# One layer of a hybrid Fourier and neighbourhood-attention block: front-stage products, low halves and the first fold given to the vector engine alone

## The chip, the cores and the metric

The kernel runs on one core of a Trainium2 chip. The engines of that core are TensorE (PE in the profile: matrix products), VectorE (DVE), ScalarE (ACT), GpSimd (POOL) and SyncE (SP, which issues most DMAs). They run side by side and wait for each other through semaphores. The metric is the device time of one execution in microseconds (us).

## The reference

One layer, one batch, 1024 positions of 1024 channels, 256 context tokens, all in fp32. Condensed:

```python
sh_x, sc_x, g_x = split(silu(c)     @ w_ada + b_ada, 3)
sh_c, sc_c, g_c = split(silu(c_ctx) @ w_ada + b_ada, 3)
xn = rms_norm(x,   norm_g) * (1 + sc_x) + sh_x
cn = rms_norm(ctx, norm_g) * (1 + sc_c) + sh_c
fx_in, fx_gate, qx, kx, vx, nx_gate = split_proj(xn @ w_in)
_, _, _, kc, vc, _                  = split_proj(cn @ w_in)
f  = real(fft2(fx_in, over positions and group channels)) * (l * 128) ** -0.5
f_out  = (f @ w_four) * silu(fx_gate)
na_out = neighbourhood_attention(rms_norm(qx), rms_norm(kx), vx, rms_norm(kc), vc, rel_bias) * silu(nx_gate)
out = x + g_x * (concat(f_out, na_out) @ w_out)
```

## The kernel before, in words

Matrix products are made of fp32 numbers cut into a high half (`h`, type fp32r) and a low half (`l`, the remainder), so that each product is three matmuls: high by high, high by low, low by high.

**The front stage** is what the change touches. Eight position tiles `x` (128 x 1024) are normalised and turned by PE into eight channel tiles, kept in `xrt` (two tensors, four channel tiles each). For each channel tile i = 0..7 the shift `sh` and the scale `av` are needed. Each is a sum of products of a row tile of the turned `w_ada` with the activated condition: `wds[i, 0]` and `wds[i, 1]` (both named `wd`, 128 x 1024) against `sbc` (for x) and `scc` (for the context). So there are 16 such dot products for x (columns `colsx`) and 16 for the context (`colsc`). `ada_out` makes three tiny instructions of the two sums of a tile (L252 to L254), and `modulate` then makes high halves `xnh` (ACT, L371), the modulated tile itself (`xrt`, ACT or DVE) and low halves `xnl` (DVE, L374). `load_gate` and its `cut` load the gate weights `wr` (128 x 512) of channel tile i and cut them into halves, both named `w`: high on ACT (L207), low by a subtraction. `gate_products` feeds PE with 24 matmuls per channel tile (L380) into the eight PSUM banks `pg`. The halves of the gate weights have three buffers, so the halves of tile i + 3 wait until PE has done the 24 matmuls of tile i.

**The fold** follows. `fourier_gate` empties `pg` into `gate_f` (ACT, L477); `fold_weights` multiplies `wtr` by `cst` into the bank `pw`, which is split into `wab_h` (ACT) and `wab_l` (DVE, L114). `fold_ends(i)` adds and subtracts mirrored positions of channel tile i: two instructions of 128 x 512, `ef` and (in place) `od`. `fold_middle` folds each once more (four DVE instructions of 128 x 256, L535, into `s`), casts to `h` on ACT (L538) and takes the low half `l` on DVE (L541, the last one L546), one step late. `fold_ends(i + 2)` stands behind the middle fold of tile i. `fold_products` gives PE 26 matmuls per tile (L554 to L567). Then `turn_columns` and everything behind it (projections, attention, output) take over.

**What sets the order.** In the front stage a planner inside the kernel runs at build time: each step has one or more alternatives (engine, guessed duration, function), and is given to the first engine that is free by the planner's own clock; the order in which the functions are called is the order on each engine. From `fold_zero` on the order is written out by the program. The planner's clock is set to zero again behind the fold, so the later stages do not depend on what it did in front.

The touched lines are L236 and L237 (scratch tiles `sq`), `far_dot` (product on POOL L288, its sum on ACT L291, or both on DVE in `dot` L257), `cut` in `load_gate` (L334 or L335), and `fold_ends` (L514, L515).

Of the kernel before, what the change touches and what calls it, by code (L numbers as in the profile page):

```python
# [11 lines left out]
F32 = mybir.dt.float32  # L12
R = mybir.dt.float32r
AF = mybir.ActivationFunctionType
ALU = mybir.AluOpType
# [4 lines left out]
P = 128  # L20
DM = 1024
KT = 8
TC, RX, RG, RM = 3.0, 2, 0, 2
TW, RT0, RT1, RT2, RH, D0, D1, NC = 4, 0, 4, -1, 1, 0, 0, 0
# [20 lines left out]
def tile_hybrid_block(  # L45
# [26 lines left out]
    act, dve, pool, pe = nc.scalar, nc.vector, nc.gpsimd, nc.tensor  # L72
# [6 lines left out]
    def f(t):  # L79
        return t.bitcast(F32)  # L80
# [35 lines left out]
    def dma(o, i):  # L116
        nc.sync.dma_start(out=o, in_=i)


    PE_, ACT_, DVE_, POOL_ = "pe", "act", "dve", "pool"  # L120
# [7 lines left out]
    def clock():  # L128
        return now[0] if past[0] is None else past[0]

    def at(t, fn):
        heapq.heappush(events, (t, len(order), fn))
        order.append(0)

    def on(alts, then=None, rank=2):

        taken = []
        for eng, dur, fn, *more in alts:
            heapq.heappush(ready[eng], (rank, len(order), dur, fn, then, more, taken))
            order.append(0)  # L140
        for eng, *_ in alts:
            issue(eng)
# [17 lines left out]
    def chain(*ops, rank=2):  # L160


        def run(n=0):
            if n == len(ops):
                return
            op = ops[n]
            if callable(op):
                at(clock() + SEM, op)
                run(n + 1)
            elif isinstance(op, list):  # L170
                on(op, lambda: run(n + 1), rank)
            else:
                on([op[:3]], lambda: run(n + 1), op[3] if len(op) > 3 else rank)
        at(clock() + (2 * SEM if past[0] is None else 0), run)

    def arrive(t, kb, fn):

        free["dma"] = max(free["dma"], t + 1.0) + 0.3643 * kb
        at(free["dma"] + 1.0, fn)
# [24 lines left out]
    def copy_by(n, who, out, in_):  # L204

        both = ((DVE_, dve.tensor_copy, lambda n: 0.07 + n * 0.00052), (POOL_, pool.tensor_copy, p_t), (ACT_, act.copy, a_t))
        return [(e, time(n), lambda cp=cp: cp(out, in_)) for e, cp, time in (both[k] for k in who)]  # L207

    def when(keys_, fn):
        if has(*keys_):  # L210
            fn()
        else:
            at(clock() + 0.1, lambda: when(keys_, fn))

    def mark(*key):
        return lambda: done.__setitem__(key if len(key) > 1 else key[0], 1)
# [15 lines left out]
    wa = st2.enter_context(tc.tile_pool(name="wa", bufs=1, **LT))  # L232
    sbc = wa.tile([P, DM], F32, name="sbc")
    scc = wa.tile([P, DM], F32, name="scc")
    junk = wa.tile([P, DM], F32, name="junk")
    sq = [wa.tile([P, DM], F32, name=f"sq{k}") for k in range(2)]  # L236
    spare = list(sq)  # L237
    sqx = w4p.tile([P, DM], F32, tag="wr", name="sqx")
    xnst = ExitStack()
    xnp = xnst.enter_context(tc.tile_pool(name="xnp", bufs=1, **RT))  # L240
# [3 lines left out]
    def halves():  # L244

        t = pwp.tile([P, 1040], R, tag="w", name="w")
        return t[:, 0:512], t[:, 512:1024]
# [8 lines left out]
    def dot(wd, s, jk, col, scale=1.0):  # L256
        dve.tensor_tensor_reduce(out=jk, in0=wd, in1=s, scale=scale, scalar=0.0, op0=ALU.mult, op1=ALU.add, accum_out=col)  # L257
# [25 lines left out]

    def far_dot(wd, s, col, key, rank):

        def product():
            scrs.append(spare.pop(0) if key[0] == "x" else wd)
            pool.tensor_tensor(out=scrs[0], in0=wd, in1=s, op=ALU.mult)  # L288

        def total():  # L290
            act.activation(scrs[0], scrs[0], AF.Copy, accum_out=col)  # L291
            if key[0] == "x":
                spare.append(scrs[0])

        scrs = []
        alts = [(DVE_, 1.14, lambda: dot(wd, s, junk, col)),
                (POOL_, 2.3, product, (ACT_, 1.04, total))]
        chain(alts[D0] if key == ("x", 0, 0) else alts[D1] if key == ("x", 0, 1) else alts, mark(*key), rank=rank)

    def ada(i, s, dsh, dav, name, rank):  # L300
        cols = wa.tile([P, 2], F32, name=f"cols{name}{i}")
        for j in range(2):
            when(((name, "s"), ("wd", i, j) if name == "x" else ("x", i, j)), lambda j=j: far_dot(wds[i, j], s, cols[:, j:j + 1], (name, i, j), rank))
        when(((name, i, 0), (name, i, 1), "vec"), lambda: chain((DVE_, 0.27, lambda: ada_out(i, cols, dsh, dav)), mark(name, i), rank=rank))
# [22 lines left out]
    def load_gate(i):  # L327
        wr = wgp.tile([P, 512], F32, tag="wr", name="wr")
        dma(wr, w_in[i * P:(i + 1) * P, 0:512])

        def cut():
            gate_w[i] = wh, wl = halves()
            chain(copy_by(512, WHO["gc"], wh, wr), mark("wh", i),
                  [(DVE_, 0.6, lambda: dve.tensor_tensor(out=wl, in0=wr, in1=f(wh), op=ALU.subtract)),  # L334
                   (POOL_, 1.22, lambda: pool.tensor_tensor(out=wl, in0=wr, in1=f(wh), op=ALU.subtract))],  # L335
                  mark("wl", i), rank=RG + 10 * i)
        arrive(clock(), 2.0, lambda: when((("g", i - 3, 2, 1),) if i > 2 else (), cut))

# [171 lines left out]
    def fold_ends(i):  # L510
        xi = xrt[i // 4][:, i % 4]
        ef = eop.tile([P, 513], F32, tag="ef", bufs=EB, name="ef")
        od = xi[:, 1:513]
        pool.tensor_tensor(out=ef[:, 1:513], in0=xi[:, 1:513], in1=xi[:, 1023:511:-1], op=ALU.add)  # L514
        pool.tensor_tensor(out=od, in0=xi[:, 1:513], in1=xi[:, 1023:511:-1], op=ALU.subtract)  # L515
        act.mul(ef[:, 0:1], xi[:, 0:1], 2.0)
        folded[i] = (ef, od)

    def fold_middle():

        lows = []
        for i in range(KT):
            ef, od = folded[i]
            h4 = pwp.tile([P, 1040], R, tag="w", name="h4")[:, 0:1024].rearrange("p (a b) -> p a b", a=4)
            l4 = eop.tile([P, 4, 256], R, tag="l4", name="l4")
            folded[i] = (h4, l4)
            lo, hi = od[:, 0:256], od[:, 510:254:-1]
            folds = (
                ((ef[:, 1:257], ef[:, 511:255:-1], ALU.add), (ef[:, 0:256], ef[:, 512:256:-1], ALU.subtract)),
                ((lo, hi, ALU.subtract), (lo, hi, ALU.add)),  # L530
            )
            for z in range(2):
                s2 = eop.tile([P, 2, 256], F32, tag="s2", bufs=3, name="s2")
                for y, (u, v, op) in enumerate(folds[z]):
                    dve.tensor_tensor(out=s2[:, y], in0=u, in1=v, op=op)  # L535
                    yield
                h, l = h4[:, 2 * z:2 * z + 2], l4[:, 2 * z:2 * z + 2]
                act.copy(h, s2)  # L538
                lows.append(dict(out=l, in0=s2, in1=f(h), op=ALU.subtract))
                if len(lows) > LAG:  # L540
                    dve.tensor_tensor(**lows.pop(0))  # L541
                yield
            if i + EB < KT:
                fold_ends(i + EB)
        for low in lows:
            dve.tensor_tensor(**low)  # L546
            yield
# [32 lines left out]
    with tc.manual_schedule(engines=MANUAL):  # L580
        fold_zero()
        for i in range(EB):
            fold_ends(i)
# [754 lines left out]
    op = {}  # L1338
# [431 lines left out]
```

## Time and profile before

| what | value |
|---|---|
| three runs, median (lowest to highest) | 627.29 us (626.17 to 630.08) |
| the profiled execution | 624.08 us, its span 622.3 us |
| busy PE / DVE / ACT / POOL | 555.5 / 494.9 / 363.6 / 294.8 us |
| mean granted TensorE clock | 0.962 of full speed |

The span is what lies between the first and the last instruction; the profiled execution's own time is 1.8 us longer. A share of busy time is an average over stages with different limits. For a change to the front stage the first 160 us are what counts: the fold's last DVE instruction starts at 146.24 us.

### The profile page before, as it was taken

The page shows a single profiled execution, that of the slowest core. Times are in us where ns is not written, and L with a number is a line of the kernel's source. Part 1 is how long each engine was busy: PE and PEld are TensorE (multiplying, and loading weights), DVE is VectorE, ACT ScalarE, POOL GpSimd, SP SyncE. Part 2 cuts the span into 40 slices and gives each one's busy share as a digit, 9 for nine tenths or more (in the row PEclk, how much of TensorE's full clock was granted, in tenths as well). Part 3 has the DMA queues.
Part 4 walks back from the last instruction along what each step waited for, and adds up shares of the span by engine and source line. Part 5 has one row for each costly group of instructions (what it writes and reads, how often), then busy time and mean ns, then how long its engine had stood idle before and what let it go on. Part 6 is the DMA issues. An engine that isn't in the chain of part 4 may idle for free. (4 is left out here: it accounts for less than half of the span.)

```text
span 622.3 us, 8690 instructions
## 1 busy us (share of the span) xinstructions
PE 555.5 (89%) x2923; PEld 482.8 (78%) x2923; DVE 494.9 (80%) x926; ACT 363.6 (58%) x765; POOL 294.8 (47%) x230
## 2 busy tenths in 40 slices
PE   6588485969999999998999989999999798999997
PEld 3466264858977798897988979889898587788886
DVE  5999999999688968868787688886868969878242
ACT  6544165525554357786688777887778737754100
POOL 3657926571374463544344553344543737515300
PEclk9889598988999999999999999999999989999999
DMA  8960033401478524112113111132011746104142
GB/s 338 407 240 0 0 112 126 137 0 61 131 234 297 160 94 123 56 38 74 34 42 109 50 55 52 41 99 61 23 46 40 230 162 214 63 5 148 52 174 97
DMA packets 42889, 68.83 MB, mean 111 GB/s; under 512 B 3542, under 2 KB 25430, under 8 KB 42844
## 3 DMA queue, kind: packets, MB, share of 16 engines
q1 hardware_dynamic: 41836, 64.60, 30.8%
q0 software_dynamic: 1008, 3.67, 1.7%
q8 instruction: 23, 0.38, 0.3%
q14 instruction: 22, 0.18, 0.1%
HBM read 59.35 MB, written 8.91 MB: 110 GB/s over the span
## 5 line engine op out<-in xcount | busy, mean ns | idle before, releaser
L812 PE MATMUL pqkv<-wh,xnh 128*128 128x384 f32 x256 | 86.8, 339 | 0.0
L812 PE MATMUL pqkv<-wl,xnh 128*128 128x384 f32 x256 | 86.7, 339 | 0.0
L812 PE MATMUL pqkv<-wh,xnl 128*128 128x384 f32 x256 | 86.1, 336 | 0.0
L1185 DVE CUSTOM_DVE_ANT_0 pr<-s,bias 128x640 f32<-128x640 f32 (+1 forms) x64 | 50.4, 787 | 22.6 <-PE s L1180 16.7
L1189 ACT ACTIVATE pr<-pr,tr 128x640 f32<-128x640 f32 (+1 forms) x64 | 51.2, 801 | 27.3 <-DVE tr L1185 26.9
L718 POOL TENSOR_TENSOR hrs<-hss,mhalf 128x4 f32<-128x4 f32 (+1 forms) x34 | 37.7, 1112 | 59.7 <-DVE hss L715 52.0
L202 DVE TENSOR_TENSOR el<-e,eh 128x384 fp32r<-128x384 f32 (+2 forms) x71 | 51.8, 735 | 11.0 <-ACT eh L207 9.9
L202 POOL TENSOR_TENSOR wl<-wr,wh 128x384 fp32r<-128x384 f32 (+1 forms) x24 | 30.4, 1271 | 46.6 <-ACT wh L207 27.8
L202 POOL TENSOR_TENSOR el<-e,eh 128x512 fp32r<-128x512 f32 x25 | 32.5, 1302 | 41.4 <-ACT eh L207 41.3
L207 ACT CAST eh<-e 128x384 fp32r<-128x384 f32 (+2 forms) x96 | 49.4, 528 | 1.4
L812 PEld LDWEIGHTS pqkv<-wl,xnh 128*128 128x128 f32 x256 | 48.1, 188 | 1.4
L812 PEld LDWEIGHTS pqkv<-wh,xnh 128*128 128x128 f32 x256 | 48.1, 188 | 1.3
L812 PEld LDWEIGHTS pqkv<-wh,xnl 128*128 128x128 f32 x256 | 48.1, 188 | 0.7
L1281 ACT ACTIVATE e<-e 128x384 f32<-128x384 f32 (+1 forms) x64 | 31.5, 496 | 29.1 <-DVE e L1271 28.6
L380 PE MATMUL pg<-xnh,w 128*128 128x512 f32 x128 | 36.9, 446 | 11.5 <-ACT xnh L371 11.5
L380 PEld LDWEIGHTS pg<-xnh,w 128*128 128x128 f32 x128 | 27.7, 220 | 20.3 <-ACT xnh L371 13.9
L1271 DVE TENSOR_TENSOR e<-st,biast 128x256 f32<-128x256 f32 (+2 forms) x80 | 34.0, 444 | 7.7 <-PE st L1263 6.8
L1178 PE MATMUL s<-ks,qs 128*128 128x256 f32 (+1 forms) x128 | 30.2, 316 | 7.4 <-DVE tr L1185 7.0
L371 ACT ACTIVATE xnh<-xrt,sh,av 128x512 fp32r<-128x512 f32 x16 | 12.6, 808 | 38.7 <-DVE av L254 38.7
L1178 PEld LDWEIGHTS s<-ks,qs 128*128 128x128 f32 x128 | 23.3, 192 | 14.9 <-DVE tr L1185 11.7
L1262 PE MATMUL st<-qs,ks 128*128 128x512 f32 (+2 forms) x96 | 33.6, 353 | 0.3
L1263 PE MATMUL st<-qs,ks 128*128 128x512 f32 (+2 forms) x96 | 33.3, 347 | 0.0
(297 smaller groups left out, 1730.0 us busy)
## 6 DMA issues: line engine op xcount, KB each, us to landing
wd<-in_w_ada_t_dram SPq DMA_DIRECT2D x16, 512.0 KB, 9.0
wr<-in_w_in_dram SPq DMA_DIRECT2D x40, 192.0 KB, 2.8
wr<-in_w_in_dram SPq DMA_DIRECT2D x24, 256.0 KB, 3.7
x<-in_xb_dram SPq DMA_DIRECT2D x8, 512.0 KB, 6.6
wdg<-in_w_ada_t_dram SPq DMA_DIRECT2D x8, 512.0 KB, 4.1
owr<-in_w_out_dram SPq DMA_DIRECT2D x16, 256.0 KB, 3.1
y<-in_xb_dram SPq DMA_DIRECT2D x8, 512.0 KB, 6.2
out_dram<-y SPq DMA_DIRECT2D x15, 256.0 KB, 2.1
```

The costliest lines, as they stand in the source:

```text
L202: return [(e, time(n), lambda eng=eng: eng.tensor_tensor(out=out, in0=in0, in1=in1, op=op)) for e, eng, time in (both[k] for k in who)]
L207: return [(e, time(n), lambda cp=cp: cp(out, in_)) for e, cp, time in (both[k] for k in who)]
L380: mm(pg[j][hf], gate_w[i][w][:, j * P:(j + 1) * P], x[i][:, hs], start=(i == 0 and g == 0), stop=(i == KT - 1 and g == 2))
L718: lambda: pool.tensor_tensor(out=rs[:, 0:nh], in0=ss[:, 0:nh], in1=mhalf[:, 0:nh], op=ALU.pow),
L812: mm(o, x[k][:, ts_], w, start=(k == 0 and n == 0), stop=(k == KT - 1 and n == 2))
L1178: mm(o, qs1[h][:, ts_], ks1[h][:, kk], start=st, stop=sp)
L1185: dve.tensor_tensor_reduce(out=pr, in0=sv, in1=bt, scale=-1.0, scalar=3.0e38, op0=ALU.add, op1=ALU.min, accum_out=tr[:, t:t + 1])
L1189: (ACT_, a_t(nl + CTX) + 0.15, lambda: act.activation(pr, pr, AF.Exp, bias=tr[:, t:t + 1], scale=-1.0, accum_out=sm[:, t:t + 1])),
L1262: mm(s, ks1[h][:, kk], qs1[h][:, qq], start=True, stop=False)
L1263: mm(s, ks2[h][:, kk], qs2[h][:, qq], start=False, stop=True)
L1271: dve.tensor_tensor(out=ew[:, u:v], in0=s3[:, u:v], in1=mixes[p, h][0][:, blocks], op=ALU.add)
L1281: ops = [(DVE_, d_t(m), add), give, lambda: done.__setitem__(("add", p, h, kt), 1), (ACT_, a_t(m), lambda: act.activation(ew, ew, AF.Exp))]
```

## The change

All 32 dot products are made on DVE, as one fused instruction each (before, 16 of them were products on POOL followed by a sum on ACT). The low halves of all eight gate weight tiles are taken on DVE (before, two of them on POOL). The 16 instructions of the first position fold are made on DVE (before, on POOL). The two scratch tiles `sq` go away. Nothing else is edited; the planner then places some other steps differently.

```diff
-    sq = [wa.tile([P, DM], F32, name=f"sq{k}") for k in range(2)]
-    spare = list(sq)
...
     def far_dot(wd, s, col, key, rank):
 
-        def product():
-            scrs.append(spare.pop(0) if key[0] == "x" else wd)
-            pool.tensor_tensor(out=scrs[0], in0=wd, in1=s, op=ALU.mult)
-
-        def total():
-            act.activation(scrs[0], scrs[0], AF.Copy, accum_out=col)
-            if key[0] == "x":
-                spare.append(scrs[0])
-
-        scrs = []
-        alts = [(DVE_, 1.14, lambda: dot(wd, s, junk, col)),
-                (POOL_, 2.3, product, (ACT_, 1.04, total))]
-        chain(alts[D0] if key == ("x", 0, 0) else alts[D1] if key == ("x", 0, 1) else alts, mark(*key), rank=rank)
+        chain((DVE_, 1.14, lambda: dot(wd, s, junk, col)), mark(*key), rank=rank)
...
             chain(copy_by(512, WHO["gc"], wh, wr), mark("wh", i),
-                  [(DVE_, 0.6, lambda: dve.tensor_tensor(out=wl, in0=wr, in1=f(wh), op=ALU.subtract)),
-                   (POOL_, 1.22, lambda: pool.tensor_tensor(out=wl, in0=wr, in1=f(wh), op=ALU.subtract))],
+                  (DVE_, 0.6, lambda: dve.tensor_tensor(out=wl, in0=wr, in1=f(wh), op=ALU.subtract)),
                   mark("wl", i), rank=RG + 10 * i)
...
-        pool.tensor_tensor(out=ef[:, 1:513], in0=xi[:, 1:513], in1=xi[:, 1023:511:-1], op=ALU.add)
-        pool.tensor_tensor(out=od, in0=xi[:, 1:513], in1=xi[:, 1023:511:-1], op=ALU.subtract)
+        dve.tensor_tensor(out=ef[:, 1:513], in0=xi[:, 1:513], in1=xi[:, 1023:511:-1], op=ALU.add)
+        dve.tensor_tensor(out=od, in0=xi[:, 1:513], in1=xi[:, 1023:511:-1], op=ALU.subtract)
```

On POOL, from the reciprocal roots `rs` of the norm to the clearing of `a` behind the fold, this stands before (the first rows of each kind):

```order
L356 TENSOR_TENSOR rs<-ss,mhalf 128x1 x8
L335 TENSOR_TENSOR w<-wr,w 128x512
L288 TENSOR_TENSOR sq_105<-wd,sbc 128x1024
...
L288 TENSOR_TENSOR wd<-wd,scc 128x1024 x3
...
L514 TENSOR_TENSOR ef<-xrt_97 128x512
L515 TENSOR_TENSOR xrt_97<-xrt_97 128x512
```

and this is all that is left there in the changed kernel (`tab`: the transform's tables; `wf`: two sums of the Fourier weights):

```order
L341 TENSOR_TENSOR rs<-ss,mhalf 128x1 x8
L560 DMA tab<-in_tab_h_dram 128x1026
L560 DMA tab<-in_tab_l_dram 128x1026
L560 DMA tab<-in_tab_h_dram 128x1026
L560 DMA tab<-in_tab_l_dram 128x1026
L595 TENSOR_TENSOR wf<-wf 128x1024
L597 TENSOR_TENSOR wf<-wf 128x1024
L625 MEMSET a_1213 64x260
```

34 instructions are gone from POOL; the two sums of `wf` now follow the table loads directly.

On DVE, at the end of the context's dot products and the start of the fold, this stands before (`x0h`: position zero; a dot is the ISA row with `junk`, the ISA row behind it reads its sum):

```order
L257 ISA junk,colsc_430<-wd,scc 128x1024
L257 ISA colsc_430 128x1
...
L254 TENSOR_TENSOR avc<-colsc_430,vec 128x1
L535 TENSOR_TENSOR s_791<-ef 128x256 x2
L535 TENSOR_TENSOR s_798<-xrt_97 128x256 x2
L541 TENSOR_TENSOR l_790<-s_791,h_789 128x512
L535 TENSOR_TENSOR s_812<-ef 128x256 x2
```

and this in the changed kernel:

```order
L255 ISA junk,colsc_424<-wd,scc 128x1024
L255 ISA colsc_424 128x1
...
L252 TENSOR_TENSOR avc<-colsc_424,vec 128x1
L499 TENSOR_TENSOR ef<-xrt_97 128x512
L500 TENSOR_TENSOR xrt_97<-xrt_97 128x512
...
L520 TENSOR_TENSOR s_773<-ef 128x256 x2
L520 TENSOR_TENSOR s_780<-xrt_97 128x256 x2
L526 TENSOR_TENSOR l_772<-s_773,h_771 128x512
L499 TENSOR_TENSOR ef<-xrt_97 128x512
L500 TENSOR_TENSOR xrt_97<-xrt_97 128x512
```

All 16 dots of the context now stand on DVE behind the last dot for x and ahead of the first fold (before, seven of the 16 were on DVE at all), and the first folds stand between the middle folds.

On ACT, at channel tiles 1 to 3, with the engines that each row waits for, this stands before:

```order
L371 ACTIVATE xnh_119<-xrt_97,sh,av 128x16x4x8 [waits DVE_49]
L291 ACTIVATE sq_106,colsx_371<-sq_106 128x1024 [waits Pool_49]
L371 ACTIVATE xnh_119<-xrt_97,sh,av 128x16x4x8
L207 CAST w<-wr 128x512 [waits DMAHW6_49,PE_49]
L291 ACTIVATE sq_105,colsx_373<-sq_105 128x1024 [waits Pool_49]
L371 ACTIVATE xnh_120<-xrt_97,sh,av 128x16x4x8 [waits DVE_49]
```

and this in the changed kernel:

```order
L356 ACTIVATE xnh_117<-xrt_97,sh,av 128x16x4x8 [waits DVE_49]
L356 ACTIVATE xnh_117<-xrt_97,sh,av 128x16x4x8
L207 CAST w<-wr 128x512 [waits DMAHW6_49,PE_49]
L358 ACTIVATE xrt_97<-xrt_97,sh,av 128x16x32 [waits Activation_49]
L356 ACTIVATE xnh_118<-xrt_97,sh,av 128x16x4x8 [waits DVE_49]
```

The sums L291 are gone from ACT, and ACT now modulates 11 of the 16 half tiles of `xrt` itself (L358; before, three), behind a cast that waits for PE. The order on PE is the same in both kernels, and so is the order on all engines behind the fold.

## Rows read from the trace of the kernel before

**Rows 1.** Two stretches: busy us (instructions) by engine, granted TensorE clock, DMA share, GB/s.
```profile
22.00:147.00 125.00, 89.24 (x428) 73.12 (x427) 122.36 (x173) 56.07 (x106) 78.99 (x43) 0.84 0.30 106
61.00:82.00 21.00, 10.14 (x24) 6.43 (x24) 20.90 (x12) 4.81 (x8) 20.44 (x8) 0.59 0.07 25
```

**Rows 2.** DVE groups by form, 20 to 147 us: count, busy us, mean ns.
```profile
L374 DVE TENSOR_TENSOR xnl<-xrt,xnh 128x512 fp32r<-128x512 f32 x16 | 17.3, 1089 | 0.1
L252 DVE TENSOR_TENSOR sh<-colsx,vec 128x1 f32<-128x1 f32 x8 | 6.9, 863 | 0.0
```

**Rows 3.** POOL groups by form, 20 to 147 us.
```profile
L288 POOL TENSOR_TENSOR wd<-wd,scc 128x1024 f32<-128x1024 f32 x9 | 26.1, 2929 | 5.2 <-ACT scc L425 5.2
L514 POOL TENSOR_TENSOR ef<-xrt 128x512 f32<-128x512 f32 x8 | 12.9, 1610 | 26.7 <-DVE shc L252 15.3 <-DVE s L535 11.4
```

**Rows 4.** Timeline of POOL and DVE around 61 to 73 us: start, us.
```profile
61.62 19.82 POOL L288 TENSOR_TENSOR wd<-wd,scc 128x1024 f32<-128x1024 f32 x7
...
70.15 2.29 DVE L252 TENSOR_TENSOR sh<-colsx,vec 128x1 f32<-128x1 f32 x1
```

**Rows 5.** Timeline of DVE, 22 to 26 us.
```profile
22.02 0.08 DVE L257 DVE_READ_ACCUMULATOR2_ANT colsx<- 128x1 f32 x1
...
23.41 2.14 DVE L254 TENSOR_TENSOR av<-colsx,vec 128x1 f32<-128x1 f32 x1
```

**Rows 6.** Timeline of DVE, 88 to 93 us.
```profile
88.14 0.68 DVE L334 TENSOR_TENSOR w<-wr,w 128x512 fp32r<-128x512 f32 x1
88.74 0.68 DVE L374 TENSOR_TENSOR xnl<-xrt,xnh 128x512 fp32r<-128x512 f32 x1
89.35 0.15 DVE L252 TENSOR_TENSOR sh<-colsx,vec 128x1 f32<-128x1 f32 x1
...
89.73 0.15 DVE L252 TENSOR_TENSOR shc<-colsc,vec 128x1 f32<-128x1 f32 x1
...
91.65 1.22 DVE L257 CUSTOM_DVE_ANT_0 junk<-wd,scc 128x1024 f32<-128x1024 f32 x1
...
92.79 0.54 DVE L372 TENSOR_SCALAR xrt<-xrt,av,sh 128x512 f32<-128x512 f32 x1
```

**Rows 7.** Timeline of PE, 20 to 97 us: the gate products.
```profile
26.45 6.69 PE L380 MATMUL pg<-xnh,w 128*128 128x512 f32 x16 [4.28 <-ACT xnh L371]
32.98 2.03 PE L380 MATMUL pg<-xnl,w 128*128 128x512 f32 x8
...
50.84 3.90 PE L380 MATMUL pg<-xnh,w 128*128 128x512 f32 x16
...
56.43 3.83 PE L380 MATMUL pg<-xnh,w 128*128 128x512 f32 x16
```

**Rows 8.** Timeline of DVE and POOL, 127 to 135 us: the middle fold.
```profile
127.23 0.75 DVE L535 TENSOR_TENSOR s<-ef 128x256 f32<-128x256 f32 x2
127.90 0.68 DVE L541 TENSOR_TENSOR l<-s,h 128x512 fp32r<-128x512 f32 x1
...
131.10 2.52 POOL L610 TENSOR_TENSOR wf<-wf 128x1024 f32<-128x1024 f32 x1
131.34 2.83 DVE L541 TENSOR_TENSOR l<-s,h 128x512 fp32r<-128x512 f32 x1
```

**Rows 9.** Timeline, 106 to 114 us: fold weights.
```profile
108.88 1.08 ACT L477 ACTIVATE gate_f<-pg 128x512 f32<-128x512 f32 x2
...
111.42 1.35 POOL L515 TENSOR_TENSOR xrt<-xrt 128x512 f32<-128x512 f32 x1
...
111.55 2.47 DVE L114 TENSOR_TENSOR wab_l<-pw,wab_h 128x512 fp32r<-128x512 f32 x4
```

**Rows 10.** Timeline of DVE and PE at the fold's end.
```profile
146.24 0.69 DVE L546 TENSOR_TENSOR l<-s,h 128x512 fp32r<-128x512 f32 x1
...
152.41 0.28 PE L669 MATMUL pp<-onesr,a 34*4 34x258 f32 x1
```

**Rows 11.** PE in two stretches of the fold: busy us (matmuls), granted clock, DMA share, GB/s.
```profile
135.00:138.00 3.00, 3.00 (x16) 0.50 0.00 0
145.00:150.00 5.00, 5.00 (x43) 1.00 0.00 0
```

## Prediction

> **What bounds the kernel now.** I first read the busy times of the stretch from 22 to 147 us, since the change touches nothing that lies outside it. DVE is busy for 122.4 of 125.0 us there and PE for 89.2 [rows 1], so DVE sets this stretch's length. The second reading is of how that time is spent. The low half of a position tile takes 0.68 us when POOL is idle [rows 6] and 1.09 us on average [rows 2]; the addition that makes `sh`, one element per partition, takes 0.15 us alone [rows 6] and 0.86 us on average [rows 2]. From 61.62 us on POOL runs seven products in a row, 19.82 us [rows 4], and one of those one-element additions takes 2.29 us in that time [rows 4]. The mean product of this kind is 2.93 us and the mean first fold on POOL 1.61 [rows 3]. That is no work: DVE stands and waits for the POOL instruction to end, about one POOL product (19.82 / 7 = 2.83 us) per DVE instruction. In 61 to 82 us DVE is "busy" for 20.9 us with 12 instructions while PE falls to a granted clock of 0.59, and the DMA share of 0.07 leaves DMAs out as the cause [rows 1]. So POOL's help in front is paid for by the engine that bounds the stage.
>
> **The change part by part.** I add up DVE's work in the new order from 22.0 us, where the last row common to both orders ends [rows 5], by undisturbed distances from one start to the next: a subtraction of 128x512 0.60 (88.14 to 88.74), the three instructions of `ada_out` 0.38 (89.35 to 89.73) [rows 6], two middle folds 0.67, and so 0.335 each (127.23 to 127.90) [rows 8]. A dot lies between 1.14 (91.65 to 92.79) and its full 1.22 [rows 6]; I take 1.2, since many now follow each other and each waits for the one before it. An in-place scale takes less than its 0.54 [rows 6]; 0.46, with the overlap of the others.
>
> New on DVE are 16 dots (19.2), two low halves of gate weights (1.2) and the 16 first folds. No row shows a first fold on DVE: it has the size of the 0.60 subtraction and the reversed operand of the middle folds, of which two, together the same elements, take 0.67. Between 0.60 and 0.67 I take 0.60, the row of one instruction: 9.6. Together 30.0 us. Against it eight scales and one copy move to ACT: 8 x 0.46 + 0.6 = 4.3 us less.
>
> All of DVE's work from 22.0 us to the last low half of the fold is then: 30 dots 36.0; 8 gate low halves 4.8; 16 `ada_out` 6.1; 5 scales 2.3; 16 `xnl` 9.6; position zero 0.3; 16 first folds 9.6; 32 middle folds 10.7; 16 low halves 9.6; 8 `wab_l` at 2.47 / 4 = 0.62 [rows 9] 5.0. Sum 94.0 us. As a test on before: 94.0 - 30.0 + 4.3 = 68.3 us of work stand in 122.4 us of busy time [rows 1], so 54 us are waiting for POOL. The change adds 30 us of work and takes nearly all of the 54 us away.
>
> Now the waits that the new order brings.
> - *Gate tiles.* With the sums of tile 0 the `av` row comes at 22.0 + 0.60 + 0.38 = 23.0 instead of ending at 25.55 [rows 5], so PE starts near 24.0 instead of 26.45. Tile 0 took 26.45 to 35.0, half of it at the low clock; a tile at full clock takes 56.43 - 50.84 = 5.6 [rows 7]. With tile 0 as before, PE ends tile 4 at 24.0 + 8.5 + 4 x 5.7 = 55.3. DVE's work for a tile (two dots 2.4, `ada_out` 0.4, a low half 0.6, two `xnl` 1.2, at times a scale) is 4.6 to 5.1, a little less than PE's 5.6, so here PE leads: the cast of gate weights i + 3 on ACT waits for PE's tile i, and queued behind it are ACT's scales and `xnh` of later tiles, for which DVE's `xnl` wait. The last such cast waits for tile 4: 55.3 + 0.6, and behind it DVE still has 0.6 + 2.4 + 1.2 + 0.4, so its dots for x end at 60.5. By work alone (14 dots, 8 low halves, 8 `ada_out`, 4 scales, 14 `xnl`) it would be 22.0 + 16.8 + 4.8 + 3.0 + 1.8 + 8.4 = 56.8. So 3.7 us of waiting. If PE keeps its clock through tile 0, nearly all of it goes; if tile 1 is half cold too, it is 3 us more.
> - *Context dots.* No other engine is needed for these; PE and ACT stand idle beside them and nothing hides them. This is the price of the change, and it is in the sum.
> - *Fold weights.* ACT does six gate activations of 0.54 [rows 9] and three casts of about that between DVE's first `s` and the first `wab_h`, some 5 us, while DVE has about 3.5 us of its own there; with a smaller gap at the second half, 2.0 us of waiting, between 0 and 4.
> - *The two sums of `wf`* stay on POOL. In before each held a DVE instruction: 2.83 instead of 0.68 [rows 8], 2.15 each. Now they run right behind the table loads, as soon as PE has read `wtr`, beside the second half of `wab_l`. Those are not stretched: four took 2.47 us beside a running POOL fold [rows 9]; one of their inputs lies in PSUM. So the first sum is mostly free and the second is not: 2.5 us, between 0 and 4.3.
>
> The Trainium skill, "SBUF — State Buffer", in its port rules, says that a DVE instruction with two SBUF inputs contends with a GpSimd instruction that reads SBUF and that one with a single SBUF input does not, outside the two-port modes. By that rule a sum beside `wab_l` costs nothing, and the trace agrees (2.47 us for four); taken for both sums it would make the time 2.5 us less.
>
> Sum: 22.0 + 94.0 + 3.7 + 2.0 + 2.5 = 124.2, against 146.9 for the end of the last low half now (146.24 + 0.69) [rows 10]: 22.7 us earlier. From there to the product that needs `a` it is 5.5 us [rows 10]. PE's last tile now lags behind DVE because two tiles before it ran at the low clock [rows 11]; without that the casts of `w4h` and the four `ah` and `al` (all there before) fill the same 5 us, so I give this tail neither gain nor loss. Behind it the order is the same on every engine, its loads wait for buffers of this stage and so come earlier by the same amount. Nothing there works against a fixed time.
>
> The profiled execution takes 624.08 us, so 624.1 - 22.7 = 601.4. The median of the runs is 3.2 us above it, 627.29; by that, 604.6 us, which is the forecast.
>
> **The rivals.**
> - *PE cold in the fold.* In the new order PE is done with the gate tiles at about 73 us (24.0 + 8.5 + 7 x 5.7) and has next to nothing to do while DVE makes the context's dots. If the clock fell to 0.50 (1.2 GHz) there and stayed low through the fold, 26 matmuls per tile at 3.0 / 16 = 0.19 [rows 11] would take 4.9 us against DVE's 3.7 (four middle folds, two low halves, two first folds): 1.2 x 8 = 10 us are lost, 614. Against it: at full clock a tile takes 26 x 5.0 / 43 = 3.0 us [rows 11], so that PE is busy 80% of the time, and in before it was back at 1.00 at 145 us after 0.50 at 135 [rows 11].
> - *PE cold in the gate tiles.* Then each tile takes 2 x 5.6, tile 4 ends 4 x 5.6 = 22 us later, DVE's fixed order waits for it, and nothing is left of the gain: 627. Against it: PE has no gap between tiles in the new order, and came to full clock within tile 0 [rows 7].
> - *DVE's long instructions are its own.* If they are stretched by something other than POOL, DVE, the bound, gets 30.0 us more work and loses 4.3: 627 + 26 = 653, slower. The place is DVE from 22 to 147 us; it decides once less than 26 of the 54 us go away. Against it: the same one-element instruction takes 0.15 and 2.29 us, and the long one lies inside POOL's run [rows 4].
> - *The full gain.* PE warm from tile 0 and both sums beside `wab_l`: 3.7 + 2.5 more, 598.4.
>
> **How the numbers follow.** I give the forecast, with its bounds, 0.78, the full gain 0.10, the cold fold 0.06, the cold gate tiles 0.03 and the slower one 0.03. The forecast's own bounds: gate tiles -3.7 or +3, first folds 0 or +1.1, dots -1.8 (at 1.14) or +0.6, fold weights -2 or +2, sums -2.5 or +1.8, runs -1.1 to +2.8 around their median. These do not fall together; I take -6 and +7, 598.5 to 611.5, which covers the forecast and the most of the full gain, about 0.85. One per cent, some 6.3 us, is what a measurement of this kernel can tell from no change. Faster by more: 0.78 + 0.10 + 0.06 = 0.94, less 0.02 for the ends of the forecast, 0.92. Within it: 0.05. Slower: 0.03.
>
> **What would show it.** In the profile of the changed kernel: no `sh` or `av` row above 0.5 us between 22 and 90 us; 16 dots for the context back to back on DVE from about 61 to 84 us with POOL empty; first folds of 0.7 us; the last low half of the fold near 124 us, PE's product with `a` near 130; from there the same distances as now. It is wrong if dots or folds on DVE cost more than their rows here, if the PE clock falls to half in the gate tiles, or if the span behind the fold grows.

## The result, and the profile after

| kernel | median (lowest to highest), runs | against the kernel before, beside it |
|---|---|---|
| before | 628.22 us (626.17 to 630.08), 4 | |
| changed | 605.41 us (601.05 to 608.82), 4 | ratio 0.9634 (95% interval 0.9554 to 0.9714) |

The change makes the kernel faster by 3.7%; 604.6 us were forecast. The profiled execution took 601.05 us, the least of the four, its span 599.3 us, 23.0 us less than before.

The stretches after, with the columns of [rows 1]:

```profile
22.00:125.00 103.00, 82.57 (x456) 71.17 (x455) 98.59 (x216) 47.58 (x86) 8.62 (x10) 0.92 0.36 129
...
61.00:85.00 24.00, 12.75 (x55) 10.46 (x54) 23.45 (x63) 1.47 (x5) 0.00 (x0) 0.79 0.42 136
```

DVE still sets the length of the stage, 98.6 of 103 us, but in 61 to 85 us it now gets through 63 instructions in 23.5 us, where [rows 1] had 12 in 20.9. The groups of DVE by form answer to [rows 2]: `xnl` is down from 1089 to 685 ns and `sh` from 863 to 151.

```profile
L359 DVE TENSOR_TENSOR xnl<-xrt,xnh 128x512 fp32r<-128x512 f32 x16 | 10.5, 685 | 0.0
...
L250 DVE TENSOR_TENSOR sh<-colsx,vec 128x1 f32<-128x1 f32 x8 | 1.2, 151 | 0.0
```

The timeline of DVE has the steps that the prediction named: the first `av` (against [rows 5]), the first sum for the context, the last one and the first folds behind it, and the last low half (against [rows 10]). The third number in brackets, where there is one, is idle time before the row and what ended it.

```profile
23.01 0.16 DVE L252 TENSOR_TENSOR av<-colsx,vec 128x1 f32<-128x1 f32 x1
...
58.60 1.22 DVE L255 CUSTOM_DVE_ANT_0 junk<-wd,scc 128x1024 f32<-128x1024 f32 x1
...
82.72 0.16 DVE L252 TENSOR_TENSOR avc<-colsc,vec 128x1 f32<-128x1 f32 x1
82.80 0.69 DVE L499 TENSOR_TENSOR ef<-xrt 128x512 f32<-128x512 f32 x1
83.52 0.69 DVE L500 TENSOR_TENSOR xrt<-xrt 128x512 f32<-128x512 f32 x1
84.12 0.69 DVE L499 TENSOR_TENSOR ef<-xrt 128x512 f32<-128x512 f32 x1
...
91.43 2.48 DVE L114 TENSOR_TENSOR wab_l<-pw,wab_h 128x512 fp32r<-128x512 f32 x4 [0.91 <-ACT wab_h L113]
...
94.73 2.48 DVE L114 TENSOR_TENSOR wab_l<-pw,wab_h 128x512 fp32r<-128x512 f32 x4 [0.48 <-ACT wab_h L113]
97.13 3.60 DVE L526 TENSOR_TENSOR l<-s,h 128x512 fp32r<-128x512 f32 x1
...
122.75 0.69 DVE L531 TENSOR_TENSOR l<-s,h 128x512 fp32r<-128x512 f32 x1
```

The timeline of POOL holds two instructions of this stage that read two tiles, against 34 more before:

```profile
95.46 2.42 POOL L595 TENSOR_TENSOR wf<-wf 128x1024 f32<-128x1024 f32 x1
97.84 2.34 POOL L597 TENSOR_TENSOR wf<-wf 128x1024 f32<-128x1024 f32 x1
```

And the timeline of PE, with the first gate tile [rows 7] and the product that needs `a` [rows 10]:

```profile
24.07 4.00 PE L365 MATMUL pg<-xnh,w 128*128 128x512 f32 x16 [1.82 <-ACT xnh L356]
27.91 2.03 PE L365 MATMUL pg<-xnl,w 128*128 128x512 f32 x8
...
128.00 0.28 PE L654 MATMUL pp<-onesr,a 34*4 34x258 f32 x1 [0.72 <-DVE a L637]
```

The last low half ends at 122.75 + 0.69 = 123.44 us, forecast 124.2, before 146.93: 23.5 us earlier. The product with `a` starts at 128.00 in place of 152.41, 24.4 us earlier. From there to the end of the span it is 471.3 us, before 469.9, so behind the fold this execution took 1.4 us longer.

### The profile page after: what moved, and what is told of

It reads as the page before. It is cut to its first block, busy times and chain, and to the rows that moved or that the text cites. A ratio compares the mean times of both kernels' runs of the same rounds, so it can differ in the third digit from the quotient of the medians.

```text
span 599.3 us, 8648 instructions
## 1 busy us (share of the span) xinstructions
PE 545.4 (91%) x2923; PEld 477.6 (80%) x2923; DVE 471.6 (79%) x967; ACT 353.4 (59%) x742; POOL 222.1 (37%) x196
## 5 line engine op out<-in xcount | busy, mean ns | idle before, releaser
L365 PE MATMUL pg<-xnh,w 128*128 128x512 f32 x128 | 31.3, 397 | 2.6 <-ACT xnh L356 2.6
L1443 PE MATMUL po<-oh,mh 128*128 128x512 f32 x88 | 32.3, 404 | 0.3 <-DVE gate L825 0.3
L365 PEld LDWEIGHTS pg<-xnh,w 128*128 128x128 f32 x128 | 23.9, 188 | 8.9 <-ACT xnh L356 3.3
```

Source lines behind the costliest of these rows:

```text
L365: mm(pg[j][hf], gate_w[i][w][:, j * P:(j + 1) * P], x[i][:, hs], start=(i == 0 and g == 0), stop=(i == KT - 1 and g == 2))
L1443: mm(o, mf[k][m][:, ts_], wf[hf][k][w_], start=(k == 0 and n == 0), stop=(k == 3 and n == 2))
```

## The experiments

Theory: a POOL instruction that reads two tiles holds up the DVE instructions with two inputs until it ends, and DVE sets the length of the stage. Main rival: DVE's long instructions are its own. The prices of the three parts of the change, taken from the traces of before and after, were to be tested too.

**The changed kernel once more.** No edit.

> The changed kernel once more, unchanged. Every theory expects 601 to 609 us, a ratio of 0.955 to 0.972 to the kernel before. What it is to tell: where its times differ from one another, whether the span or what lies around it differs, and whether the granted clock goes with it.

Measured: 605.89 us (603.74 to 609.17), ratio 0.9665 (0.9595 to 0.9735). The profiled execution has a span of 602.5 us. In 24 to 30 us PE had a granted clock of 0.73 where the first trace had 1.00, and the 16 products at the start of tile 0 took 5.28 us in place of 4.00; the context's part ended 0.6 us later. Of this 0.35 us is there already at the first `av` (23.36 in place of 23.01), ahead of the first gate product, which leaves 0.2 us for the lower clock. What lies around the span is 1.8 us in both. From the product with `a` to the end of the span it is 473.8 us here and 471.3 in the first trace: 2.5 of the 3.2 us between the two spans lie behind the fold, with nothing edited. What makes them was not followed up.

**The sums of products back.**

```diff
-        chain((DVE_, 1.14, lambda: dot(wd, s, junk, col)), mark(*key), rank=rank)
+        alts = [(DVE_, 1.14, lambda: dot(wd, s, junk, col)),
+                (POOL_, 2.3, product, (ACT_, 1.04, total))]
+        chain(alts[D0] if key == ("x", 0, 0) else alts[D1] if key == ("x", 0, 1) else alts, mark(*key), rank=rank)
```

> Only the sums of products for shift and scale may go to POOL again (16 of the 32 do); gate low halves and first folds stay on DVE. Theory (a POOL product of two SBUF inputs holds DVE up): nearly all of the gain is lost, since the front part, up to the last sum of products for the context, gave 21.9 of the 23 us and the fold part 1.5: 622 to 627 us. Rival (the folds on POOL were what cost): it stays within 4 us of the changed kernel, 601 to 609.

Measured: 623.30 us (621.00 to 626.97, 10 runs), ratio 0.9926 (0.9893 to 0.9958). The theory's 622 to 627. With 17 products on POOL (9 for x, 8 for the context) DVE's timeline has the old picture again, a one-element addition of 2.29 us and a one-element product of 2.14, with a one-element scale of 0.20 between them:

```profile
73.26 2.29 DVE L252 TENSOR_TENSOR sh<-colsx,vec 128x1 f32<-128x1 f32 x1
75.47 0.20 DVE L253 TENSOR_SCALAR colsx<-colsx,vec 128x1 f32<-128x1 f32 x1
75.71 2.14 DVE L254 TENSOR_TENSOR av<-colsx,vec 128x1 f32<-128x1 f32 x1
```

**The first folds back.**

```diff
-        dve.tensor_tensor(out=ef[:, 1:513], in0=xi[:, 1:513], in1=xi[:, 1023:511:-1], op=ALU.add)
-        dve.tensor_tensor(out=od, in0=xi[:, 1:513], in1=xi[:, 1023:511:-1], op=ALU.subtract)
+        pool.tensor_tensor(out=ef[:, 1:513], in0=xi[:, 1:513], in1=xi[:, 1023:511:-1], op=ALU.add)
+        pool.tensor_tensor(out=od, in0=xi[:, 1:513], in1=xi[:, 1023:511:-1], op=ALU.subtract)
```

> Only the 16 first folds go back to POOL. Theory: in the fold, DVE loses by waiting for POOL (about 0.4 us in each of 32 instructions) what it saves in folds (10.6 us), so between 0 and 4 us are lost, most likely 1.5: the two traces show 42.2 us for this part before and 40.6 after. Rival (the folds are half of the gain): 10 us or more are lost.

Measured: 610.52 us (605.29 to 611.22), ratio 0.9706 (0.9643 to 0.9769), 4.9 us above the changed kernel by the medians, so more than the 0 to 4 expected, though the interval overlaps that of the changed kernel. DVE's timeline shows what the expectation left out. The first four folds don't wait for the fold stage; POOL makes them as soon as the tiles are there, from 79.87 us on, beside the last tiles of the context, and four one-element instructions take 1.2 us:

```profile
80.92 1.22 DVE L250 TENSOR_TENSOR shc<-colsc,vec 128x1 f32<-128x1 f32 x1
...
85.92 1.19 DVE L252 TENSOR_TENSOR avc<-colsc,vec 128x1 f32<-128x1 f32 x1
87.03 0.75 DVE L520 TENSOR_TENSOR s<-ef 128x256 f32<-128x256 f32 x2
```

So the context's part ends at 87.03 in place of 82.80, 4.2 us later, and from there the fold takes 42.2 us (its last low half ends at 129.22), as it did before, against 40.6. My 1.5 us was only the second of these; the first I had counted with the sums of products.

**The gate weights' low halves back.**

```diff
-                  (DVE_, 0.6, lambda: dve.tensor_tensor(out=wl, in0=wr, in1=f(wh), op=ALU.subtract)),
+                  [(DVE_, 0.6, lambda: dve.tensor_tensor(out=wl, in0=wr, in1=f(wh), op=ALU.subtract)),
+                   (POOL_, 1.22, lambda: pool.tensor_tensor(out=wl, in0=wr, in1=f(wh), op=ALU.subtract))],
```

> Only the low halves of the gate weights may go to POOL again (all eight do). Theory: a POOL subtraction of 128x512 holds one DVE instruction for about 1.2 us, while DVE saves 0.6 us each, and in the gate tiles PE leads DVE by a little: 0 to 3 us lost. Rival (less work on DVE is a gain even so): 0 to 5 us gained.

Measured: 609.60 us (607.50 to 611.73), ratio 0.9710 (0.9654 to 0.9766), some 4 us above the changed kernel by the medians, with overlapping intervals: the sign of the theory, a little over its 3 us. All eight subtractions went to POOL (1843 ns on average, where 1.2 us were expected), the mean `xnl` rose from 685 to 1027 ns, and the first `avc` came 5.05 us later. Not all of that is the price of the subtractions: this execution was 0.5 us behind at the norm's `rs` already, and PE had a granted clock of 0.50 in 24 to 30 us.

**Unneeded products on POOL.** This takes DVE's work out of the comparison: DVE does what it does in the changed kernel, in the same order.

```diff
+        def extra():
+            if key[0] == "c" and key[2] == 0:
+                pool.tensor_copy(tiny, col)
+                pool.tensor_tensor(out=scr, in0=wd, in1=s, op=ALU.mult)
+            done[key] = 1
-        chain((DVE_, 1.14, lambda: dot(wd, s, junk, col)), mark(*key), rank=rank)
+        chain((DVE_, 1.14, lambda: dot(wd, s, junk, col)), extra, rank=rank)
```

> The changed kernel, and on POOL, behind the first sum of products of each of the context's eight tiles, a one-element copy and one product of 128x1024 that nothing reads. DVE's and ACT's own instructions and their order stay as they are, so DVE gets no work. Theory (a POOL product of two SBUF inputs holds the next DVE instruction of two SBUF inputs until it ends): each of the eight costs DVE 1.3 to 2.6 us, so the context's part gets 10 to 21 us longer and the time comes to 616 to 627. Rival (DVE's long instructions are its own): 605, within 3.

Measured: 622.28 us (621.19 to 626.21), ratio 0.9906 (0.9851 to 0.9961). The last `avc` ends at 101.67 us in place of 82.88, 18.8 us later. The first 1.35 us of this were lost ahead of the first unneeded product: the first sum for the context starts at 59.95 in place of 58.60, with PE at a granted clock of 0.54 in 24 to 30 us. From that sum on it is 41.7 us against 24.3, 17.4 us more: 2.18 us for each of the eight products. In DVE's timeline, a sum of products that meets an unneeded product takes 3.38 us, and the one after it, with POOL idle, 1.23:

```profile
59.95 1.22 DVE L257 CUSTOM_DVE_ANT_0 junk<-wd,scc 128x1024 f32<-128x1024 f32 x1
...
72.99 3.38 DVE L257 CUSTOM_DVE_ANT_0 junk<-wd,scc 128x1024 f32<-128x1024 f32 x1
...
76.42 1.23 DVE L257 CUSTOM_DVE_ANT_0 junk<-wd,scc 128x1024 f32<-128x1024 f32 x1
...
101.51 0.16 DVE L254 TENSOR_TENSOR avc<-colsc,vec 128x1 f32<-128x1 f32 x1
```

POOL's timeline has the product beside the first of them:

```profile
72.95 2.34 POOL L289 TENSOR_TENSOR scr<-wd,scc 128x1024 f32<-128x1024 f32 x1
```

The DVE instruction starts 0.04 us behind POOL's and ends 1.08 us behind its end (76.37 against 75.29), so it did nearly all of its own work after POOL had ended. That DVE's long instructions are its own is thereby excluded: nobody reads these products, and DVE got no instruction more. The Trainium skill, "SBUF — State Buffer", section "SBUF: two separate sides", says that such a pair of instructions excludes each other for the whole length of one, and does not share bandwidth; the 3.38 us agree with that.

**Fills in place of products.**

```diff
-                pool.tensor_tensor(out=scr, in0=wd, in1=s, op=ALU.mult)
+                pool.memset(scr, 0.0); pool.memset(scr, 1.0)
```

> As the run with idle products, but each product replaced by two fills of the same 128x1024 scratch tile with a constant: POOL writes SBUF for about as long and reads nothing. Theory (it is POOL's reading of SBUF that holds DVE): 605, within 3, and no addition of one element above 0.5 us. Rival (any POOL instruction that uses SBUF holds DVE): 8 to 16 us more, 613 to 621.

Measured: 606.88 us (605.85 to 607.88), ratio 0.9650 (0.9603 to 0.9697). POOL is busy for 21.6 of the 24 us from 61 to 85, and DVE's sums and additions keep their lengths, as a sum and the two fills beside it show (timelines of DVE and POOL):

```profile
66.42 1.23 DVE L257 CUSTOM_DVE_ANT_0 junk<-wd,scc 128x1024 f32<-128x1024 f32 x1
66.36 1.97 POOL L289 MEMSET scr<- 128x1024 f32 x2
```

It is POOL's reading that holds them. Whether reading one tile is enough is not shown: every long POOL instruction of this stage, in all these runs, reads two inputs or none.

**Fills in the kernel before.**

```diff
-            pool.tensor_tensor(out=scrs[0], in0=wd, in1=s, op=ALU.mult)
+            [pool.memset(scrs[0], v) for v in (1.0, 0.0)]
```

> The kernel before, with each of POOL's 16 products for shift and scale replaced by two fills of the tile that the product would have written. It leaves out the multiplication of 16 of the 32 sums of products, whose sums are thus wrong. Instructions, order and waits on every engine stay as before. Theory (DVE loses by POOL's reads): the context's part ends near 75 us instead of 104.7, and the time is 594 to 604. Rival (the front waits for the sums on ACT, behind POOL, so the work that went round by POOL and ACT set the time): above 618.

Measured: 597.59 us (595.43 to 599.62), ratio 0.9502 (0.9451 to 0.9553). The last `avc` ends at 76.86 us in place of 104.65, in DVE's timeline before and with fills:

```profile
104.49 0.16 DVE L254 TENSOR_TENSOR avc<-colsc,vec 128x1 f32<-128x1 f32 x1
76.70 0.16 DVE L254 TENSOR_TENSOR avc<-colsc,vec 128x1 f32<-128x1 f32 x1
```

With the same instructions on DVE, 27.8 us go from the front once POOL doesn't read. POOL's own road is not quite the same, as the expectation had it: the fills don't wait for `scc` on ACT (5.2 us before), and those for the last seven products take 14.18 us in place of 19.82. That this shorter road made the gain is excluded by the trace before: from 22 to 147 us DVE was idle for 2.6 us in all, 1.6 of it in waits for ACT, and none of these waits was for a sum. The run also shows what the change pays: with 16 sums of products more on DVE the changed kernel needs 82.88 us to that point, 6.0 more (6.7 counted from the norm's `rs`, which came 0.7 us later with the fills).

**Part of the context's sums late.** Four kernels take the context's tiles from 4, 6 or 7 on out of the front and make their sums behind the fold, from weights loaded again; two of them have the edit of the run that follows as well. The core of the edit:

```diff
-        when((("h", 0, 1),), lambda: ada(i, scc, shc, avc, "c", 200 + i))
+        if i < 4:
+            when((("h", 0, 1),), lambda: ada(i, scc, shc, avc, "c", 200 + i))
...
+    def late_dot(n):
+        i, j = n // 2, n % 2
+        wd = w4p.tile([P, DM], F32, tag="wr", name="wdc")
+        dma(wd, w_ada_t[(8 * j + i) * P:(8 * j + i + 1) * P, :])
+        ops = [(DVE_, 1.15, lambda: dot(wd, scc2, wd, colc[:, n:n + 1]))]
...
```

From tile 4:

> The changed kernel, with the context's tiles 4 to 7 taken out of the front: their eight sums of products and four sets of shift and scale run behind the fold, where DVE has some 12 us of slack, from weights loaded a second time. Theory (the context's sums of products stand bare on the path in front): 8 x 1.2 + 4 x 0.38 = 11.1 us go from the front, and some or none of it comes back behind the fold: 594 to 606. Rival (they fill a wait for something else, or are paid back in full behind): 605 or more.

From tile 6, and from tiles 6 and 7 together with the edit of the run that follows:

> As the run with tiles 4 to 7 late, but only the context's tiles 6 and 7: four sums of products and two sets of shift and scale, 4 x 1.2 + 2 x 0.38 = 5.6 us, leave the front; 2.5 MB in place of 4.5 MB are loaded a second time. Theory (what broke the other was the second load, in front of w_in): the loads now fit beside w_in's, the fold ends 3 to 5.6 us earlier, and the time is 599 to 604. Rival (any load or wait put there costs as much as it saves): 605 to 615.

> Tiles 6 and 7 late and the two sums of wf on DVE. If both edits do what their theories say and add up: the fold ends 6 to 8 us earlier than in the changed kernel, 596 to 602 us. If the late loads cost what they save: 603 to 613.

> Only tile 7 late (two sums of products, one set of shift and scale, 2.8 us; 1.5 MB loaded a second time) and the two sums of wf on DVE. If they add up: 4 to 5 us less than the changed kernel, 600 to 602. If any late load costs what it saves: 603 to 608.

| late from | last `avc` made in front ends | last low half of the fold ends | median (lowest to highest) | ratio (interval) |
|---|---|---|---|---|
| none (changed kernel) | 82.88 | 123.44 | 605.41 (601.05 to 608.82) | 0.9634 (0.9554 to 0.9714) |
| 4 | 72.55 | 114.32 | 625.48 (623.93 to 626.48) | 0.9944 (0.9895 to 0.9992) |
| 6 | 77.53 | 119.21 | 621.50 (619.52 to 623.42) | 0.9899 (0.9861 to 0.9937) |
| 6, sums of `wf` on DVE | 77.83 | 116.18 | 619.13 (617.06 to 620.42) | 0.9854 (0.9816 to 0.9892) |
| 7, sums of `wf` on DVE | 81.18 | 119.52 | 613.91 (612.36 to 614.92) | 0.9773 (0.9736 to 0.9810) |

In front the theory holds. From the first sum for the context to the last `avc` made in front it is 13.1 us without the last four tiles, 18.7 without two and 21.5 without one, against 24.3 in the changed kernel: 11.2, 5.6 and 2.8 us less, and 11.1, 5.6 and 2.8 were expected. So the context's sums do stand bare on the path. Behind the fold all of it is lost, and two to four times as much again. The waits between 114 and 200 us of the kernel with tiles 4 to 7 late (us in total, times, longest) show the nearest cause, products that wait for a low half of `w_in` and casts that wait for its loads:

```profile
PE pqkv L801 <- DVE wl L202: 20.2, 1, 20.2
ACT wh L207 <- DMA wr<-in_w_in_dram: 19.8, 8, 5.9
```

In the changed kernel the second of these waits is 5.4 us, from 120 to 200 us, and the first is not among PE's longest there. The edit also takes buffers from two tiles there and lets the planner order that stage anew; which of the second loads, the buffers and the order costs what was not told apart. The hope that two tiles, or one, would fit was wrong: the last three kernels came out above both ranges that were given for them.

**The two sums of `wf` on DVE.** The last POOL products of the stage, moved to where DVE waits for ACT.

```diff
         for n in range(PW):
+            if n == 0:
+                dve.tensor_tensor(out=wfr[0], in0=wfr[0], in1=wfr[1], op=ALU.add)
+            if n == 4:
+                dve.tensor_tensor(out=wfr[2], in0=wfr[2], in1=wfr[1], op=ALU.subtract)
             weights_next(n)
...
-            if i == WL:
-                pool.tensor_tensor(out=wfr[0], in0=wfr[0], in1=wfr[1], op=ALU.add)
-            if i == WL + 1:
-                pool.tensor_tensor(out=wfr[2], in0=wfr[2], in1=wfr[1], op=ALU.subtract)
```

> The changed kernel, with the last two POOL products of the fold, the two sums of wf, on DVE, each ahead of four low halves wab_l, where DVE waits for ACT's casts (0.91 and 0.48 us in the changed kernel). Theory (each wait hides part of its sum, and no POOL instruction holds DVE any more): DVE pays 1.14 - 0.91 and 1.14 - 0.48, 0.9 us, in place of the 2.9 us that the low half beside the second sum loses, so the last low half ends 2.0 us earlier, near 121.4 us, and the time is 0.5 to 3 us less. Rival (the casts come later too, so the sums are paid in full): 2.3 against 2.9 us, no change within 1 us.

Measured: 602.80 us (597.63 to 606.01, 6 runs), ratio 0.9590 (0.9543 to 0.9637). DVE's timeline:

```profile
84.14 0.69 DVE L499 TENSOR_TENSOR ef<-xrt 128x512 f32<-128x512 f32 x1
...
91.79 1.22 DVE L581 TENSOR_TENSOR wf<-wf 128x1024 f32<-128x1024 f32 x1
92.93 2.48 DVE L114 TENSOR_TENSOR wab_l<-pw,wab_h 128x512 fp32r<-128x512 f32 x4
...
95.66 1.22 DVE L583 TENSOR_TENSOR wf<-wf 128x1024 f32<-128x1024 f32 x1
96.79 2.48 DVE L114 TENSOR_TENSOR wab_l<-pw,wab_h 128x512 fp32r<-128x512 f32 x4
99.19 0.68 DVE L526 TENSOR_TENSOR l<-s,h 128x512 fp32r<-128x512 f32 x1
...
121.89 0.69 DVE L531 TENSOR_TENSOR l<-s,h 128x512 fp32r<-128x512 f32 x1
```

The waits of 0.91 and 0.48 us are filled, and the low half behind them takes 0.68 in place of 3.60. From the first fold to the last low half it is 121.89 - 84.14 = 37.75 us against 122.75 - 82.80 = 39.95 (40.02 when the changed kernel ran again): 2.2 us less, 2.0 expected. The end itself came only 0.86 us earlier, since this execution reached the fold 1.3 us later: it was 0.4 us behind at the first `av`, and lost the rest in the gate tiles, the first of which it ran at a granted clock of 0.61. Its median is the lowest of all kernels with the full computation; the two intervals overlap, so that it beats the changed kernel is shown by the fold's own length and not by the times.

## Why the prediction was right

**The reason.** That DVE's "busy" time held some 54 us of waiting for POOL was the right reading. Products that nobody reads bring 2.18 us each back, fills bring none to the sums and additions, and fills in the kernel before take 27.8 us away. The slower rival is excluded by the first of these. The trace after agrees with the size: DVE is busy for 97.3 us from 22 us to the end of the last low half, of which 2.9 are the low half that still meets a POOL product. Less the 31.0 us that the change put on DVE (19.2 for sums of products, 1.2 for low halves, 10.6 for first folds), and with the 4.3 us that went to ACT, 67.7 us of the 122.4 before were work, and 54.7 waiting.

**The parts.** Taken back one at a time, the sums of products cost 17.7 us (623.30 - 605.65, the middle of the two medians of the changed kernel), the first folds 4.9 and the low halves 3.9, together 26.5 where the medians of the whole change differ by 22.8. The planner gave all eight low halves to POOL, not the two of before; whether the rest of the difference is an overlap of the parts or the scatter of the medians is not shown.

**The terms.**

| step | forecast | measured |
|---|---|---|
| gate tiles: DVE's waits | 3.7 | 0.88 + 0.56 = 1.4 |
| x part ends | 60.5 | 58.60 |
| context's part, bare | 24.3 | 82.80 - 58.60 = 24.2 |
| 16 first folds | 9.6 | 8 x (0.72 + 0.60) = 10.6 |
| fold weights: waits | 2.0 | 0.91 + 0.48 = 1.4 |
| two sums of `wf` | 2.5 | 3.60 - 0.69 = 2.9 |
| last low half ends | 124.2 | 123.44 |
| from there to the product with `a` | 5.5 | 128.00 - 123.44 = 4.6 |
| behind it | as before | 1.4 longer (some 4 when the kernel ran again) |

- *Gate tiles* was the term most off, by its condition and not by its mechanism. I took tile 0 as half cold, as in [rows 7]; in the profiled execution PE ran it at a granted clock of 1.00 from 24 to 30 us (before 0.63), as the full-gain rival had it. The order of DVE's work up to the first sum for the context is the same in the runs with idle products and with `wf` on DVE, and from the first `av` to that sum it took 35.6 us at 1.00, 35.8 at 0.73 (the changed kernel again), 36.5 at 0.61 and 37.2 at 0.54, with a first tile of 8.3 us in the last of them. The forecast, with a first tile of 8.5 us, has 60.5 - 23.0 = 37.5. So the term was right for a cold first tile, and the clock of the execution decided how much of it came.
- *First folds.* A fold with a reversed operand takes 0.69 us, as the subtraction does, but the second of a pair, which writes in place what the first reads, starts 0.72 us behind the first, and only the next instruction starts 0.60 behind it. The upper bound of 1.1 us more was nearly right.
- *The sums of `wf`.* The first was free beside `wab_l` and the second held a low half, as forecast.
- *Context's part.* Nothing hid it, as forecast, but the passage has PE idle beside it, and PE made gate products until 70.1 us.
- *The cold rivals.* The granted clock fell to 0.79 in 61 to 85 us and was 0.91 in 85 to 125; it cost DVE no wait, since no row of DVE in the fold waits for PE.
- *Behind the fold* I had said that nothing changes, and that a longer span there would be a sign of being wrong. It was 1.4 us longer, but two executions of the changed kernel differ there by 2.5 us, so one trace of each kernel doesn't tell whether the change cost anything there.

The errors nearly cancel: -2.0 in front, +1.2 in the fold, -0.9 in the tail, +1.4 behind, 601.05 against 601.4 in the profiled execution. The medians differ from it by 4.4 us now and by 3.2 before, hence 605.4 against 604.6. That the forecast comes within 1 us is luck, then; that the terms of the front and the fold are each right to 2 us is not.

## What to carry to other kernels

A busy engine may be waiting: compare an instruction's duration with the same form at a moment when the other engine is idle, and take a one-element instruction as the probe, since what it lasts beyond 0.15 us is no work. Where the engine that sets a stage's length shares its reads with a helper, count what the helper's instruction takes from it (here 2.18 us for each POOL product of 2.34 us, against 1.2 us for doing the work itself). Work that can't leave the path may still fit into a wait on it, as the two sums did; moved to a later stage with a second load, in the one form tried, it cost more than it saved.

## What the runs showed of the hardware

- A scale and shift of 128x512 on DVE, with one tile as input, is held even by a fill. In the run with fills it takes 1.29 us beside one (0.54 in the changed kernel; 2.76 beside a product, in the run with idle products), and that is most of the 0.8 us by which the context's part ended later; in the kernel before with fills its mean is 817 ns. The two timelines (DVE and POOL of the run with fills):

```profile
61.03 1.29 DVE L365 TENSOR_SCALAR xrt<-xrt,av,sh 128x512 f32<-128x512 f32 x1
61.09 2.12 POOL L289 MEMSET scr<- 128x1024 f32 x2
```

  A form's number of inputs alone does not tell: the two-input sums beside the same fills kept their 1.22 us. The Trainium skill, "SBUF — State Buffer", section "SBUF: two separate sides", counts a DVE instruction in a two-port mode as in conflict with any GpSimd instruction, and one with two SBUF inputs only with one that reads. Both rows agree, if the held form ran in such a mode, which no row shows.
- It goes the other way too. The one-element copy on POOL took 0.18 us when DVE was between its sums (run with idle products) and 0.95 to 1.24 us beside one (1.24 at 59.91 us in the run with fills).
- The granted clock of the first gate tile differed between executions of the same kernel (1.00 and 0.73 from 24 to 30 us), with PE idle for the same 1.82 us before it; with idle products it was 0.54, after 1.82 us again. No row shows what decides it.
